# Attention results without transfers, and a new written order of the attention stage, in a one-core transformer block

## The chip, the cores and the metric

The kernel runs on one core of one Trainium2 chip. Its time is the device time of one launch, in microseconds (us), and the number compared is the median over several runs. A core has five instruction queues that work at the same time, each strictly in the order in which its program stands: TensorE (PE in the profile, with its weight loads as PEld), VectorE (DVE), ScalarE (ACT), GpSimd (POOL) and SyncE (SP). Here SP issues most of the DMA transfers. Matmul results land in PSUM, which DVE and ACT read; all other data lies in SBUF, or in DRAM between stages.

## What is computed

The input is one sequence of 1024 frames with 1024 features. One layer is computed in float32:

```
h = rms_norm(x, norm1);  proj = h @ w_in          -> q, k, v for 8 + 8 heads of 64, forget gates, gates
o_a = forgetting attention, 8 heads, causal:  softmax(q k^T/8 + c_t - c_s) v
o_b = band attention, 8 heads: own chunk of 64 frames and the 8 chunks before it, plus a learned bias by distance
merged = sigmoid(g_a) * (o_a @ w_branch_a) + sigmoid(g_b) * (o_b @ w_branch_b)
x = x + merged @ w_out
x = x + square(relu(rms_norm(x, norm2) @ w_up)) @ w_down
return rms_norm(x, final_norm)
```

## The kernel before

**Precision.** The matmuls take operands of the type F32R, so each float32 operand is split into a high half (a rounding copy, name ends in `h`) and a low half (the rest, name ends in `l`), and a product takes three matmuls: high by high, low by high, high by low. ACT makes high halves and DVE or POOL the low ones.

**Stages.** Projections of q, k, v and gates (to some 420 us), attention with pieces of the branch product laid into it (some 420 to 670 us), the rest of the branch product (to 717 us), the output product (to 793 us), and the two feed-forward products. The change touches only the attention and its two ends.

**Attention.** The sixteen heads run in the order of the list `HEADS`: number n = 0 to 7 are the eight forgetting ("fox") heads, 8 to 15 the eight band heads. Two heads that follow each other form a pair `pr`, and lie in rows 0 to 63 (`hh` = 0) and 64 to 127 (`hh` = 1) of one result tile. For a head there are eight chunks of 128 queries: scores into a PSUM tile `s` (there are two of these, used in turn), minimum over the keys on DVE into `mn`, exponential on ACT into `p<chunk>`. Then, for the two halves h of the queries, PE turns blocks of `p` (matmul against `ident`, into `pt`), ACT rounds them (`th`), DVE takes the low part (`tl`), and PE weighs the values with both into one PSUM tile `pv`. Rows 0 to 63 of `pv` hold the part from the low halves of the values, rows 64 to 127 that from the high halves; the result is their sum.

**The order** is written out by hand. Strings of letters stand for calls: `S` scores of the next chunk, `R` its minimum, `E` its exponential, `T` turn a group, `H` and `L` its two halves, `P` weigh it, `V` take the result out of `pv`, `F` one step of the branch product for the fox half of the heads ("filler": three matmuls), `M` the end of a group of four such steps, `O` the split of a finished band result. `FOX_HEAD` is the string of a fox head, `BAND_HEAD` of a band head (its F and M are left out before n = 9), `LAST_HEAD` of head 15, and `INTRO` moves the first letters of head 0 forward. Engines see the letters in this order, since the calls are kept in program order (`tc.keep_in_program_order`; SP's transfers called by `LO` too). `S`, `R`, `E` run one head ahead: while head n is turned and weighed, the chunks of head n + 1 are scored. The first chunks of head 0 are scored already between the last gate products, how many beside each is in `AHEAD`.

**The result of a half head** goes out in `evacuate`: ACT copies `pv` to `both`, SP sends rows 64 to 127 of it to the result tile `on` and rows 0 to 63 to the tile `lo`, so that both stand in the rows of the head. When a pair is whole, `done` adds `lo` to `on` for both halves on POOL, fetches the spread reciprocals of the softmax sums (`rb`, through DRAM: `reciprocals`, `spread_reciprocals`) and `normalise` multiplies. For fox pairs POOL also splits the product into `oh` and `ol`, which the fillers and the branch product read; band pairs go through DRAM (`o_dram`, back as `olt`), except the last one, which is split into `o3h` and `o3l`. Head 15 goes another way: ACT copies one half, DVE adds the other.

**The branch product's weights** for the band half (`ab_weight(0, c)`) are loaded and split after the written order, where the scheduler finds room.

Of the kernel before, what the change touches and what calls it, by code (L numbers as in the profile page):

```python
# [34 lines left out]
EARLY, AHEAD = 3, (0, 0, 0, 0, 2, 2, 2, 1)  # L35
# [5 lines left out]
INTRO = "THLPTHLTTHPHLL"  # L41
FOX_HEAD = "THSSRRETTSLPHEHTLSRTLPHERPHTSLTELSHVTPHRLRELTHSEPTSHLRPEPPLPHRLEPV"
BAND_HEAD = "FFTSFHTHFRLSLRMPETSHETPLFRHETSPLRHFVSTPEHLTRHPLLSFETFPRHLESPPSMRRVEE"
LAST_HEAD = "THLTHLFFFFMTHPPFLFFFMTPTHFLHFTFFPVLTMHPFHLTHFFFLPLOOOPOOMOPV"
# [47 lines left out]
def hybrid_block(ctx: ExitStack, tc: tile.TileContext, xT, xN, g1, wall, wf, fb, relb, g2, g3, outT):  # L92
# [567 lines left out]
    def make_scores():  # L660
        if len(made) == len(chunks):
            return
        n, i = chunks[len(made)]
        made.append(pss.tile([P, S], F32, tag="s", name="s"))
        score(n, i, made[-1], TO)
        if i == 7 and n + 2 < 16:
            load_head(n + 2, LO)
# [29 lines left out]
    oh = opool.tile([P, 4, S], F32R, tag="oh", name="oh")  # L697
    ol = opool.tile([P, 4, S], F32R, tag="ol", name="ol")
    o3h, o3l = [opool.tile([P, S], F32R, tag=t, name=t) for t in ("o3h", "o3l")]
# [25 lines left out]
    def fill():  # L725
# [28 lines left out]
        for n, (c, h) in enumerate(todo):  # L754
# [5 lines left out]
            for k in range(4):  # L760
                product(ps, k == 0, [((wh[:, k, :], wl[:, k, :]), (oh[:, k, hs(h)], ol[:, k, hs(h)]))], k < 3, TO)
# [32 lines left out]
    evac = []  # L794

    def weigh(n, h, js, first, last):
# [11 lines left out]
        if last:  # L808
            rows = slice(hh * HD, (hh + 1) * HD)
            if hh == 0:  # L810
                outs[pr, h] = ap0.tile([P, HALF], F32, tag="on", name=f"on{pr}_{h}", bufs=4)
                lows_o[pr, h] = ap0.tile([P, HALF], F32, tag="lo", name=f"lo{pr}_{h}", bufs=3)
            evac.append((n, h, pv))

    def evacuate():
            n, h, pv = evac.pop(0)
            pr, hh = HEADS[n]
            rows = slice(hh * HD, (hh + 1) * HD)
            if n == 15:
                AO.copy(lows_o[pr, h][rows], pv[0:HD])  # L820
                VO.tensor_tensor(outs[pr, h][rows], pv[HD:P], lows_o[pr, h][rows], op=ALU.add)
                done(n, h)
                return
            both = ap0.tile([P, HALF], F32, tag="both", name=f"both{n}_{h}", bufs=2)
# [3 lines left out]
            done(n, h)  # L828
            if n == 14:
                G.tensor_tensor(outs[pr, h][rows], outs[pr, h][rows], lows_o[pr, h][rows], op=ALU.add)  # L830
# [487 lines left out]
```

## Time and profile before

| what | us |
|---|---|
| median of 3 runs | 1441.51 (1438.96 to 1443.76) |
| profiled execution, its own time | 1437.3 |
| span of the profiled execution, first to last instruction | 1435.6 |
| PE busy in it | 1398.8 (97%) |
| DVE, ACT, POOL busy | 872.1, 698.1, 825.9 |
| mean granted clock of PE | 0.993 |

In the rows of the profile, `out<-in` names the tiles written and read, `x` gives a count of instructions in a row that groups several. In a timeline row the first number is the start in us from the start of the span, the second the length; a bracket at the end tells how long the engine sat idle before it and what ended that wait. In a row by stretches of time there stand the stretch, its length, then for PE, PEld, DVE, ACT and POOL the busy time and in brackets the instructions, then the clock that PE was granted (1.00 is full), the busy share of the DMA engines, and what they moved in GB/s. Matmuls overlap: the next one starts some time before the one ahead is shown to end, so what a matmul costs the queue is read from start to start.

### The profile page before, as it was taken

To read this page: it belongs to the slowest core of one execution; us is meant where nothing else is said; L and a number is where in the kernel's file an instruction comes from. 1 tells how busy PE (TensorE), PEld (TensorE's weight loads), DVE (VectorE), ACT (ScalarE), POOL (GpSimd) and SP (SyncE) were. 2 spreads that over 40 slices of the span, in tenths; PEclk is the share of its full clock that TensorE was granted. 3 is DMA by queue.
4 is the path that set the end of the run, shared out by engine and by line. 5 is a ranking of instruction groups with operands and counts; after the bars stand their busy time and mean duration, and the time that the engine had idled before them with its cause. 6 is when DMAs were issued, how large, how long until landed. Compare 5 with 4: busy or idle time off the path is not lost.

```text
span 1435.6 us, 20509 instructions
## 1 busy us (share of the span) xinstructions
PE 1398.8 (97%) x6658; PEld 1167.0 (81%) x6658; DVE 872.1 (61%) x1369; ACT 698.1 (49%) x1349; POOL 825.9 (58%) x650
## 2 busy tenths in 40 slices
PE   7999999999989999999999999999999999999996
PEld 5788888888878888887888788888888888888886
DVE  7756445543258886775655854554545558998644
ACT  8633333343348886764454543333343444444653
POOL 1377777779730433233833777777777546567563
PEclk9999999999999999999999999999999999999998
DMA  8447677773456898997644244444445784679263
GB/s 277 148 113 197 185 202 207 205 192 128 146 187 173 232 261 231 270 278 247 206 167 154 67 156 155 154 159 149 152 143 180 245 266 153 178 240 234 81 220 118
DMA packets 137622, 267.64 MB, mean 186 GB/s; under 512 B 19554, under 2 KB 21602, under 8 KB 134442
## 3 DMA queue, kind: packets, MB, share of 16 engines
q1 hardware_dynamic: 89658, 181.19, 41.0%
q10 hardware_dynamic: 44656, 77.26, 17.0%
q0 software_dynamic: 3200, 7.88, 2.5%
q8 instruction: 52, 0.85, 0.2%
q14 instruction: 56, 0.46, 0.1%
HBM read 172.70 MB, written 85.69 MB: 180 GB/s over the span
## 4 chain that ended last, share of the span: by engine, by line
PE 84%; DVE 4%; issue 3%; DMA 3%; POOL 2%; ACT 2%; SPq 1%; POOLq 0%; ACTq 0%; DVEq 0%
PE u L215 42%; PE dS L215 12%; PE dA L215 8%; PE o L215 5%; PE s L105 4%; PE m L215 3%; PE pt L105 3%; PE pv L105 3%; PE m L105 2%; PE u L105 1%; DMA wr<-wall 1%; DMA lo<-both 1%; DMA rb<-r_dram 1%; DVE s L105 1%; ACT th L105 1%
## 5 line engine op out<-in xcount | busy, mean ns | idle before, releaser
L164 POOL TENSOR_TENSOR wl_A<-wr,wh_A 128x512 fp32r<-128x512 f32 x118 | 158.5, 1352 | 90.5 <-ACT wh_A L162 75.0
L164 POOL TENSOR_TENSOR wl_S<-S,wh_S 128x512 fp32r<-128x512 f32 x102 | 136.2, 1338 | 30.9 <-ACT wh_S L162 30.3
L162 ACT CAST wh_S<-S 128x512 fp32r<-128x512 f32 x105 | 64.8, 621 | 115.4 <-PE u L215 58.7
L162 ACT CAST wh_A<-wr 128x512 fp32r<-128x512 f32 x105 | 64.9, 620 | 89.1 <-PE u L215 43.5
L905 POOL TENSOR_TENSOR on<-on,lo 128x512 f32<-128x512 f32 x14 | 18.0, 1288 | 156.8 <-DMA lo<-both 66.4
L105 DVE TENSOR_TENSOR tl<-pt,th 128x512 fp32r<-128x512 f32 (+1 forms) x144 | 91.0, 642 | 21.4 <-ACT th L105 20.6
L164 POOL TENSOR_TENSOR wl_S<-ks,wh_S 128x512 fp32r<-128x512 f32 x48 | 69.0, 1486 | 52.5 <-ACT wh_S L105 51.2
L105 ACT CAST th<-pt 128x512 fp32r<-128x512 f32 (+1 forms) x144 | 79.4, 554 | 35.0 <-PE pt L105 34.1
L578 DVE TENSOR_TENSOR u<-u,u 128x512 f32<-128x512 f32 x70 | 48.8, 697 | 75.8 <-PE u L215 73.2
L105 ACT ACTIVATE p<-s,mn 128x640 f32<-128x640 f32 (+4 forms) x121 | 85.9, 710 | 14.9 <-DVE mn L105 13.2
L105 PE MATMUL pt<-ident,p 128*128 128x128 f32 x528 | 81.0, 275 | 0.0
L185 POOL TENSOR_TENSOR S<-wr,wr 128x512 f32<-128x512 f32 x35 | 46.1, 1317 | 57.8 <-DMA wr<-wall 57.7
L105 PEld LDWEIGHTS pt<-ident,p 128*128 128x128 f32 x528 | 65.7, 142 | 11.1 <-issue 0.4
L164 POOL TENSOR_TENSOR wl_A<-ka,wh_A 128x512 fp32r<-128x512 f32 x32 | 45.8, 1439 | 35.6 <-ACT wh_A L105 34.3
L105 PE MATMUL pv<-th,v 128*128 128x512 f32 (+3 forms) x180 | 61.8, 353 | 3.1 <-ACT th L105 3.1
L277 ACT CAST qkh<-qk 128x512 fp32r<-128x512 f32 x32 | 19.9, 621 | 88.5 <-DMA sk_dram<-qkl 31.8
L105 PE MATMUL s<-qk 128*128 128x384 f32 (+2 forms) x192 | 60.5, 370 | 1.9 <-ACT p L105 1.8
L1073 ACT ACTIVATE v<-v 128x512 f32<-128x512 f32 x64 | 40.4, 632 | 44.6 <-DVE v L1072 42.1
L571 DVE TENSOR_TENSOR u<-u,c 128x512 f32<-128x512 f32 x35 | 24.5, 699 | 57.5 <-PE u L215 55.4
L105 PE MATMUL pv<-tl,v 128*128 128x512 f32 (+3 forms) x180 | 57.7, 339 | 1.3 <-DVE tl L105 1.3
L105 DVE CUSTOM_DVE_ANT_0 s<-s,bc 128x640 f32<-128x640 f32 (+2 forms) x64 | 42.3, 661 | 24.7 <-PE s L105 17.6
L1072 DVE SCALAR_TENSOR_TENSOR v<-u,rstd 128x512 f32<-128x512 f32 x64 | 43.9, 688 | 20.1 <-PE u L215 18.1
(437 smaller groups left out, 4703.6 us busy)
## 6 DMA issues: line engine op xcount, KB each, us to landing
wr<-wall SPq DMA_DIRECT2D x235, 256.0 KB, 3.5
a_dram<-at ACTq DMA_DIRECT2D x64, 256.0 KB, 2.0
xT<-a_dram SPq DMA_DIRECT2D x64, 256.0 KB, 4.1
qk<-qk_dram SPq DMA_DIRECT2D x15, 1024.0 KB, 5.3
qk_dram<-qkh ACTq DMA_DIRECT2D x96, 128.0 KB, 2.4
a_dram<-v ACTq DMA_DIRECT2D x48, 256.0 KB, 2.0
xB<-a_dram SPq DMA_DIRECT2D x44, 256.0 KB, 5.3
z_dram<-zt ACTq DMA_DIRECT2D x32, 256.0 KB, 2.5
```

Of the source, the lines that this page charges most:

```text
L105: return lambda *a, **kw: tc.keep_in_program_order(getattr(self.eng, name)(*a, **kw))
L162: (act.tensor_copy if act is G else act.copy)(wh, src)
L164: lows.append(eng.tensor_tensor(wl, src, wh.bitcast(F32), op=ALU.subtract))
L185: eng.tensor_tensor(t, raw(3), raw(2), op=ALU.add)
L215: done = eng.matmul(bank, w[wi], x[xi], start=(first and t == 0), stop=(t == n - 1 and not part), skip_group_check=part or not first)
L277: A.copy(dst[0], src)
L571: V.tensor_tensor(banks[1], banks[3], c22, op=ALU.add)
L578: V.tensor_tensor(banks[b], banks[b], u2, op=ALU.add)
L905: G.tensor_tensor(o, o, lows_o[pr, x], op=ALU.add)
L1072: V.scalar_tensor_tensor(v, src, 0.0, rstd[:, hs(h)], op0=ALU.max, op1=ALU.mult)
L1073: A.activation(v, v, AF.Square)
```

## The change

1. **No transfers of results.** `evacuate` is cut in two. `V` is one copy of 64 rows on ACT, which also moves them into the rows of the head; a new letter `X` (`evacuate_rest`) is the second step. For the first half (h = 0) of heads 0 to 13 that is a second ACT copy, into `lo`, and POOL adds the two later, once for a pair. For the second half, and for heads 14 and 15, ACT copies one half to `mv` and DVE adds the other straight from `pv`. The two transfers of each half head are gone.
2. **Reciprocals earlier.** They are taken at the first weighing of the pair's second head, fetched at its first half (with one transfer where there were two), and each half is normalised when it is there.
3. **The eighth chunk of head 0** is scored beside the seventh, ahead of the last gate product.
4. **New strings** for all four parts.
5. **Branch weights in the string.** A new letter `W` splits the first four weights of `ab_weight(0, c)` in the last head; they are loaded at filler steps 36, 40, 44 and 52.
6. `oh`, `ol`, `o3h`, `o3l` are one tile for each half, and the loads at the start of attention stand in another order (values of head 0 first, then heads 1 and 2).

```diff
-EARLY, AHEAD = 3, (0, 0, 0, 0, 2, 2, 2, 1)
+EARLY, AHEAD = 3, (0, 0, 0, 0, 2, 2, 2, 2)
-FOX_HEAD = "THSSRRETTSLPHEHTLSRTLPHERPHTSLTELSHVTPHRLRELTHSEPTSHLRPEPPLPHRLEPV"
+FOX_HEAD = "STTHRSETSHLRLREPTHLPTHESHLPVTRTELSRXHTLHSPEPHLTPTSHRLPEPHLRLESPRPVXE"
...
     def evacuate():
-            AO.copy(both, pv)
-            LO.dma_start(outs[pr, h][rows], both[HD:P])
-            LO.dma_start(lows_o[pr, h][rows], both[0:HD])
-            done(n, h)
+        if n == 15 and h:
+            normalise(pr, 0)
+        if h == 0 and n < 14:
+            AO.copy(outs[pr, h][rows], pv[HD:P])
+        else:
+            moved[n, h] = ap0.tile([P, HALF], F32, tag="mv", name=f"mv{n}_{h}", bufs=2)
+            AO.copy(moved[n, h][rows], pv[other])
+
+    def evacuate_rest():
+        n, h, pv = evac.pop(0)
...
+        if h == 0 and n < 14:
+            AO.copy(lows_o[pr][rows], pv[0:HD])
+        else:
+            VO.tensor_tensor(outs[pr, h][rows], pv[rows], moved.pop((n, h))[rows], op=ALU.add)
+        done(n, h)
...
     def spread_reciprocals(pr):
-        for hh in range(2):
-            LO.dma_start(rb[hh * HD:(hh + 1) * HD, :], r_dram[pr, hh:hh + 1, :].to_broadcast([HD, S]))
+        LO.dma_start(rb, r_dram[pr].rearrange("a (o s) -> a o s", o=1).to_broadcast([2, HD, S]))
...
+    load_values(0)
     load_head(1, LO)
-    load_values(0)
+    load_head(2, LO)
     load_values(1)
...
-        if js == order[0] and hh and h == int(n < 15):
+        if js == order[0] and hh and h == 0:
             reciprocals(pr)
...
-        elif h and hh:
-            for x in range(2):
-                o = outs[pr, x]
-                G.tensor_tensor(o, o, lows_o[pr, x], op=ALU.add)
-            spread_reciprocals(pr)
-            for x in range(2):
-                normalise(pr, x)
+        elif hh:
+            if h == 0:
+                o = outs[pr, h]
+                G.tensor_tensor(o, o, lows_o[pr], op=ALU.add)
+                spread_reciprocals(pr)
+            normalise(pr, h)
...
+        if fill_at in (36, 40, 44, 52):
+            c = len(branch_raw) + len([b for b, _ in ab_w if b == 0])
+            branch_raw.append(quarter(U_AB + c // 2, (0, 3)[c % 2], LO.dma_start))
...
+    def branch_weight():
+        AO.copy(wh, raw)
+        G.tensor_tensor(wl, raw, wh.bitcast(F32), op=ALU.subtract)
```

What the strings do to the queues is shown at two places; the names are the program's, with a running number behind a tile's name.

**PE at the start of attention.** `u7_3` is the last gate product (twelve matmuls), `s_4098` and `s_4034` are the scores of the eighth chunk of head 0. Before:

```order
L105 MATMUL u7_3_3682<-T4h_104,wl_7_A22_3918 128x512
L105 MATMUL s_4098<-qk0_3799 128x512 x2
L105 MATMUL s_4098<-sk0_3800 128x512 x2
L105 MATMUL pt_4110<-ident_66,p0_0_3943 128x128
L105 MATMUL pt_4110<-ident_66,p0_1_3949 128x128
L105 MATMUL pt_4110<-ident_66,p0_2_3971 128x128
L105 MATMUL pt_4110<-ident_66,p0_3_3977 128x128
L105 MATMUL pv_4119<-th_4111,v0_4094 128x512
L105 MATMUL pv_4119<-tl_4112,v0_4094 128x512
```

After the change, where the rows of `s_4034` stand before the first of the twelve matmuls of `u7_3`, and the last of these is followed by:

```order
L105 MATMUL u7_3_3682<-T4h_104,wl_7_A22_3918 128x512
L105 MATMUL pt_4114<-ident_66,p0_0_3943 128x128
L105 MATMUL pt_4114<-ident_66,p0_1_3949 128x128
L105 MATMUL pt_4114<-ident_66,p0_2_3971 128x128
L105 MATMUL pt_4114<-ident_66,p0_3_3977 128x128
L105 MATMUL pt_4121<-ident_66,p0_1_3949 128x128
L105 MATMUL pt_4121<-ident_66,p0_2_3971 128x128
L105 MATMUL pt_4121<-ident_66,p0_3_3977 128x128 x2
L105 MATMUL pt_4128<-ident_66,p0_2_3971 128x128
L105 MATMUL pt_4128<-ident_66,p0_3_3977 128x128
L105 MATMUL pv_4138<-th_4115,v0_4099 128x512
L105 MATMUL pv_4138<-tl_4116,v0_4099 128x512
```

The scores moved ahead of the gate product, and three turned groups stand before the first weighing, where it was one.

**PE where one fox head passes into the next.** `s_4257` and `s_4273` are the scores of the eighth chunk of the head that is being scored; the rows run from there. Before, the five weighings of the last five groups come behind it, of which the first four are:

```order
L105 MATMUL s_4257<-qk1_4087 128x512 x2
L105 MATMUL s_4257<-sk1_4088 128x512 x2
L105 MATMUL pv_4225<-th_4187,v0_4094 128x512
L105 MATMUL pv_4225<-tl_4188,v0_4094 128x512
L105 MATMUL pv_4225<-th_4199,v0_4094 128x512
L105 MATMUL pv_4225<-tl_4200,v0_4094 128x512
L105 MATMUL pv_4225<-th_4219,v0_4094 128x512
L105 MATMUL pv_4225<-tl_4220,v0_4094 128x512
L105 MATMUL pv_4225<-th_4236,v0_4094 128x384
L105 MATMUL pv_4225<-tl_4237,v0_4094 128x384
L105 MATMUL pv_4225<-th_4236,v0_4094 128x128
L105 MATMUL pv_4225<-tl_4237,v0_4094 128x128
```

After:

```order
L105 MATMUL s_4273<-qk1_4101 128x512 x2
L105 MATMUL s_4273<-sk1_4102 128x512 x2
L105 MATMUL pv_4230<-th_4240,v0_4099 128x384
L105 MATMUL pv_4230<-tl_4241,v0_4099 128x384
L105 MATMUL pv_4230<-th_4240,v0_4099 128x128
L105 MATMUL pv_4230<-tl_4241,v0_4099 128x128
L105 MATMUL pv_4230<-th_4249,v0_4099 128x256
L105 MATMUL pv_4230<-tl_4250,v0_4099 128x256
L105 MATMUL s_4297<-qk2_4108 128x128
L105 MATMUL s_4297<-sk0_3800 128x128
```

Only the last two groups are weighed behind the eighth chunk now; the first chunk of the next head (`s_4297`) follows, then two turned groups of four blocks, then the second chunk. Before, one turned group and the first chunk came behind the last weighing, and the second chunk right after.

**ACT at the same place**, one head later. `p_7` is the exponential of the eighth chunk. Before:

```order
L105 ACTIVATE p_6_4857,den_4705<-s,mn_4702 128x896
L105 CAST th<-pt 128x256
L105 ACTIVATE p_7_4871,den_4705<-s,mn_4702 128x1024
L105 COPY both_1_4877<-pv 128x512
L105 CAST th<-pt 128x512
L105 ACTIVATE p_0_4909,den_4705<-s,mn_4906 128x128
```

After:

```order
L105 CAST th<-pt 128x256
L105 ACTIVATE p_6_4850,den_4702<-s,mn_4697 128x896
L105 COPY mv_1_4870<-pv 64x512
L105 ACTIVATE p_7_4876,den_4702<-s,mn_4697 128x1024
L105 CAST th<-pt 128x512
L105 ACTIVATE p_0_4901,den_4702<-s,mn_4896 128x128
```

The copy out of `pv`, which waits for the last weighing, stands ahead of the eighth exponential now, and stood behind it.

More of the change, by code (lines that the diff above doesn't have):

```diff
@@ L696, in hybrid_block @@
     opool = pool(ostack, "opool", "left")
-    oh = opool.tile([P, 4, S], F32R, tag="oh", name="oh")
-    ol = opool.tile([P, 4, S], F32R, tag="ol", name="ol")
-    o3h, o3l = [opool.tile([P, S], F32R, tag=t, name=t) for t in ("o3h", "o3l")]
+    ohl = [[opool.tile([P, 4, HALF], F32R, tag=f"o{t}{h}", name=f"o{t}{h}") for t in "hl"] for h in range(2)]
+    o3 = [[opool.tile([P, HALF], F32R, tag=f"o3{t}{h}", name=f"o3{t}{h}") for t in "hl"] for h in range(2)]
     apq.append(pool(astack, "apq1", "right"))
@@ L792, in turn_p @@
         return pt[:, :x], th[:, :x], tl[:, :x]
-    evac = []
+    evac, moved = [], {}
     def weigh(n, h, js, first, last):
@@ L952, in branch @@
         wh, wl = ab_weight(0, c)
-        xs = [(oh[:, k, hs(h)], ol[:, k, hs(h)]) for k in range(3)] + [(o3h[:, hs(h)], o3l[:, hs(h)])]
+        xs = [(ohl[h][0][:, k, :], ohl[h][1][:, k, :]) for k in range(3)] + [o3[h]]
         product(ps, 0 in ks, [((wh[:, k, :], wl[:, k, :]), xs[k]) for k in ks], 3 not in ks)
```

60 lines of the change are left out of this document (29 added, 31 removed).

## The prediction

> **What bounds the kernel now.** I read the page's totals first, then the table by stretches of time, stage by stage.
>
> ```profile
> span 1435.6 us, 20509 instructions
> PE 1398.8 (97%) x6658; PEld 1167.0 (81%) x6658; DVE 872.1 (61%) x1369; ACT 698.1 (49%) x1349; POOL 825.9 (58%) x650
> ```
>
> PE is busy for 97% of the span, and the change takes no matmul away. So a gain can only come out of the 36.8 us in which PE sits idle, and out of time in which it runs at less than its full clock; a loss is a new wait of PE. By stretches, three places in the attention stage stand out:
>
> ```profile
> core 0: us, PE busy (x) PEld busy (x) DVE busy (x) ACT busy (x) POOL busy (x), PEclk, DMA share, GB/s
> 420.00:424.00 4.00, 1.03 (x7) 0.66 (x5) 2.30 (x4) 1.63 (x3) 0.00 (x0) 1.00 0.56 154
> 424.00:428.00 4.00, 3.36 (x19) 2.49 (x20) 2.27 (x4) 1.40 (x4) 0.00 (x0) 1.00 0.51 207
> 428.00:432.00 4.00, 3.29 (x14) 2.56 (x14) 2.20 (x9) 2.02 (x7) 0.00 (x0) 0.70 0.51 133
> 432.00:436.00 4.00, 4.00 (x27) 3.78 (x26) 3.09 (x7) 3.70 (x9) 0.00 (x0) 0.87 0.19 44
> 459.70:473.00 13.30, 13.14 (x86) 11.68 (x85) 11.43 (x29) 11.77 (x29) 7.46 (x7) 1.00 0.87 235
> 548.00:552.00 4.00, 1.03 (x6) 0.48 (x4) 1.39 (x2) 1.26 (x4) 4.00 (x5) 1.00 1.07 400
> 552.00:556.00 4.00, 3.83 (x15) 3.29 (x15) 1.68 (x5) 0.84 (x3) 2.60 (x3) 0.57 0.98 208
> 664.00:668.00 4.00, 3.22 (x17) 2.46 (x15) 0.88 (x2) 2.47 (x5) 1.84 (x2) 1.00 1.02 369
> 668.00:672.00 4.00, 1.59 (x7) 1.11 (x7) 4.00 (x4) 3.98 (x8) 2.30 (x2) 1.00 0.88 302
> 672.00:676.00 4.00, 3.83 (x10) 2.69 (x11) 3.87 (x8) 0.02 (x1) 0.00 (x0) 0.58 0.77 234
> ```
>
> Each place costs twice: the idle time, and then a stretch at about half the clock. Start of attention: idle 2.97 + 0.64 + 0.71 = 4.32, clock 4 x 0.30 + 4 x 0.13 = 1.72, together 6.0 us. First fillers: idle 2.97 + 0.17 = 3.14, clock 4 x 0.43 = 1.72, together 4.9. End of attention: idle 0.78 + 2.41 + 0.17 = 3.36, clock 4 x 0.42 = 1.68, together 5.0. That is 15.9 us on offer. The row from 459.70 is one fox head: PE 13.14 of 13.30, with ACT and DVE not far behind.
>
> **Start of attention (-4.0).** The rows of the three engines:
>
> ```profile
> 419.51 0.62 PE L105 MATMUL s<-qk 128*128 128x512 f32 x2
> 420.43 0.60 PE L105 MATMUL pt<-ident,p 128*128 128x128 f32 x4
> 421.05 1.22 DVE L105 CUSTOM_DVE_ANT_0 s<-s,wide 128x1024 f32<-128x1024 f32 x1
> 422.37 1.11 ACT L105 ACTIVATE p<-s,mn 128x1024 f32<-128x1024 f32 x1 [3.03 <-DVE mn L105]
> 424.10 0.49 PE L105 MATMUL pv<-th,v 128*128 128x512 f32 x1 [3.07 <-ACT th L105]
> 419.71 0.70 DVE L578 TENSOR_TENSOR u<-u,u 128x512 f32<-128x512 f32 x1 [0.96 <-PE u L105]
> 420.44 0.69 DVE L391 TENSOR_TENSOR zt<-u,rstd 128x512 f32<-128x512 f32 x1
> ```
>
> PE waits for `th`, which stands on ACT behind the eighth exponential, which waits for the eighth minimum, which waits for scores that PE has only just made. Scored before the last gate product, that chain of 1.32 (start of minimum to start of exponential) + 1.11 lies beside twelve gate matmuls, and `th` can start at once. Late next are the last gate's two DVE steps: the gate product ends 0.92 later (419.51 to 420.43, the scores that now stand ahead of it), so they end near 422.0, and the third turned group and the first `tl` stand behind them. That is about 1.2 of waiting; some 0.8 more I leave for the eight chunks of head 1, which are now scored with little else between. So 2.0 of 6.0 stay and no half-clock stretch. Ends: 1.7 gained (the clock alone) and 6.0.
>
> **First fillers (-4.9).**
>
> ```profile
> 550.39 0.50 PE L105 MATMUL m<-oh,wh_ab 128*128 128x512 f32 x1 [1.86 <-POOL oh L860]
> 552.17 0.55 PE L105 MATMUL m<-ol,wh_ab 128*128 128x512 f32 x1 [1.28 <-POOL ol L861]
> 547.28 2.51 POOL L855 TENSOR_TENSOR on<-on,rb 128x512 f32<-128x512 f32 x2 [0.94 <-DMA rb<-r_dram]
> rb<-r_dram SPq DMA_DIRECT2D x16, 256.0 KB, 6.9
> L105 SPq DMA_DIRECT2D on<-both x30: 461/477/605, 434.0 to 649.1; - x30
> ```
>
> PE waits for `oh` of the last fox pair, POOL for `rb`, and `rb` for an SP queue full of result transfers. With the change the reciprocals leave half a head earlier, and the first half is added and normalised in the middle of head 7: by the string some 6 us ahead of the head's end, with all of head 8 (about 13) before the first filler, against the 6.9 that `rb` takes to land in the median and four POOL steps of at most 1.3 (two took 2.51). I take the whole 4.9. Ends: 0 (if `rb` lands after all that) and 5.3.
>
> The transfers themselves (60 issues on SP, the 30 of `on` of 0.477 each in the median, and as many of `lo`) were on no other wait of PE, so I count nothing more for them. The four weight loads moved onto SP at steps 36 to 52 are issued in its program order, between result transfers that are gone: nothing.
>
> **End of attention (-4.4).**
>
> ```profile
> 669.87 0.45 PE L105 MATMUL s<-tl,v 128*128 128x384 f32 x1 [2.11 <-DVE tl L105]
> 665.46 1.31 ACT L162 CAST wh_ab<-wr 128x512 fp32r<-128x512 f32 x2 [2.80 <-DMA wr<-wall]
> ```
>
> The last `th` stands on ACT behind two weight splits that wait 2.80 for a load, and `tl` behind that. With `W` the loads are issued a head ahead, and the last two `th` stand ahead of what could still be late (the second set of `olt`, and the fourth `W` behind it). I leave 0.6 of the 5.0 for the last `tl` and the first split results. Ends: 0 gained and 5.0.
>
> **The seams of the fox heads (+6.0).** The price of the new order lies here. One seam now:
>
> ```profile
> 464.83 0.40 PE L105 MATMUL pv<-th,v 128*128 128x512 f32 x1
> 466.21 0.33 PE L105 MATMUL pv<-th,v 128*128 128x384 f32 x1
> 467.02 0.60 PE L105 MATMUL pt<-ident,p 128*128 128x128 f32 x4
> 467.37 0.31 PE L105 MATMUL s<-qk 128*128 128x128 f32 x1
> 467.51 0.27 PE L105 MATMUL s<-sk 96*128 96x128 f32 x1
> 467.71 0.39 PE L105 MATMUL s<-qk 128*128 128x256 f32 x1
> 468.05 0.82 PE L105 MATMUL pt<-ident,p 128*128 128x128 f32 x6
> 469.03 0.44 PE L105 MATMUL s<-qk 128*128 128x384 f32 x1 [0.16 <-ACT p L105]
> 466.45 1.12 ACT L105 ACTIVATE p<-s,mn 128x1024 f32<-128x1024 f32 x1 [0.32 <-DVE mn L105]
> 467.55 0.58 ACT L105 COPY both<-pv 128x512 f32<-128x512 f32 x1
> ```
>
> The scores of the eighth chunk leave PE at 464.83, and the second chunk of the next head takes the same tile of `s` as soon as the eighth exponential has read it: 467.57 ends ACT, 467.71 starts PE. That chain cannot be shorter than some 0.2 (PE to DVE) + 1.32 + 1.12 + 0.14 = 2.78. Now it is nearly covered: of the 2.88 from 464.83 to 467.71 PE waits about 0.14, and then about 0.45 for the third chunk (six turned blocks from 468.05 take 0.53, so it could start at 468.58). In the new order the cover is two weighings (466.21 to 467.02: 0.81), the first chunk (0.2) and two turned groups (0.35 each): 1.7. So PE waits 1.1, and for the third chunk, whose tile is freed by an exponential behind the eighth one and a rounding, about 0.35. Against 0.59 now, 0.85 more at each of seven seams between fox heads; the eighth, where the band chunks are shorter, little: 6.0 together. The ends: 0 (some other waits of a head vanish as the order shifts) and 10, if the copy out of `pv`, now ahead of the eighth exponential on ACT, adds its 0.58 each time. I take 6.0, by the row of the chain itself, which no other engine can shorten.
>
> **Added instructions.** Per head one ACT copy and one DVE add more, priced by head 15, which does this already:
>
> ```profile
> 671.44 0.58 ACT L105 COPY lo<-s 64x512 f32<-64x512 f32 x1
> 659.23 0.69 DVE L105 TENSOR_TENSOR on<-s,lo 64x512 f32<-64x512 f32 x1 [0.58 <-ACT lo L105]
> ```
>
> In a fox head ACT goes from 11.77 to 12.35 and DVE from 11.43 to 12.12 of 13.3: both stay under PE's 13.14, so beside the seams nothing. In the band heads with fillers PE has no wait to gain or lose: nothing. POOL drops adds that nobody on PE waits for.
>
> Sum: -4.0 - 4.9 - 4.4 + 6.0 = -7.3. The profiled execution took 1437.3 (span 1435.6), 4.2 below the median of 1441.51; I take the change off the median: 1441.5 - 7.3 = 1434.2, say **1434**.
>
> **The rivals.** *The seams cost nothing* beyond what they cost now: then -13.3, about 1428. For it: ACT and DVE have over 1 us to spare in a head. Against: the chain above is one of lengths, not of room.
>
> *A late transfer keeps one stall*: `rb` at the first fillers, or `olt` or a weight at the end. Then 4.4 to 4.9 is not gained: about -2.7, 1439, no measurable change (0.3%, or 4.3 us, is about what a measurement of this kernel can tell from none). For it: loads and results still share SP's queue, in which an issue waits for the one ahead. Against: the half head of lead.
>
> *Slower: the clock drops at the seams.* If a seam's waits bring on a half-clock stretch of 1.7 as at the three places, eight seams cost 13.6 more: -7.3 + 13.6 = +6.3, about 1448. It decides from five such stretches on. For it: the waits of a seam grow from 0.6 to about 1.45 us, within some 2.5 us. Against it: clocks fell behind 2.97 and 2.41 of idle in 4 us, and not behind this:
>
> ```profile
> 820.00:822.00 2.00, 0.93 (x5) 0.67 (x4) 2.00 (x9) 0.94 (x3) 2.00 (x2) 1.00 0.04 13
> ```
>
> The Trainium skill, "TensorE: Matmul & The Clock Gate", bears on this from two sides. Its Part 1 on the HAM clock gate states that the clock falls after an idle window of about 3.4 us: by that no seam would bring it down, and the sum stays -7.3; but the trace shows half clock after 1.86 and 1.28 of waiting with a matmul between, so it takes less than a full empty window. Its section "A second HAM failure mode: psum-queue depth-cycling" states that frequent short idle times between groups of matmuls make the clock swing: by that the sum would be +6.3. The trace does not bear it out: the fox heads now, with two waits at each seam, show 1.00.
>
> **How the numbers follow.** The forecast holds with 0.61 (its own range 1429 to 1437), no seam cost 0.15, one stall kept 0.15, clock drops 0.09. Faster by over 0.3%: 0.61 + 0.15 = 0.76; within: 0.15; slower: 0.09. The range takes in the first three cases with the ends of seams and stalls: 1425 to 1442.
>
> **What would show it.** Right: no stretch below full clock between 420 and 680; PE at the first fillers without a wait for `oh`; fox heads of about 14.1 us where now a head is 13.3, with PE waiting for `p` at the second chunk of each; no wait of ACT for `wr` at the end. Wrong: fox heads of 13.3 (seams covered) or of over 15 (clock), a wait for `rb` on POOL that reaches PE, or ACT waiting for `olt` ahead of a `th`.

## The result: 1478.5 us, slower by 2.5%, and the profile after

The changed kernel takes 1478.47 us (1475.98 to 1480.31) against 1442.33 for the kernel before on the same chip: ratio 1.0253, interval 1.0227 to 1.0279. The forecast was 1434 and its range ended at 1442. The first part of the profile after:

```profile
span 1474.3 us, 20382 instructions
PE 1415.2 (96%) x6658; PEld 1176.5 (80%) x6658; DVE 890.9 (60%) x1385; ACT 707.9 (48%) x1363; POOL 816.0 (55%) x641
```

PE does the same 6658 matmuls. It is idle for 1474.3 - 1415.2 = 59.1 us instead of 36.8, and takes 16.4 longer over them, in line with a lower mean clock (0.980 instead of 0.993). From the table of PE's waits in the kernel after (engine, line, released by; us in total, times, longest):

```profile
PE s L105 <- DMA sk<-sk_dram: 11.3, 6, 2.3
PE s L105 <- DMA qk<-qk_dram: 6.6, 4, 3.4
...
PE s L105 <- ACT p L105: 6.2, 9, 0.9
PE m L215 <- ACT wh_ab L105: 5.2, 1, 5.2
PE m L105 <- POOL wl_ab L745: 5.1, 3, 4.2
```

The wait for `oh` and `ol` at the first fillers is gone, as forecast. Four of these five lines are new, and they do not name the seams: they name head loads (`qk`, `sk`) and weight halves. The wait for `p` is the seams', and small. Of POOL's waits the longest in total is now this one:

```profile
POOL on L860 <- DMA rb<-r_dram: 127.3, 7, 23.6
```

Before, POOL waited 7.9 us for `rb` in all. The timeline of the kernel after around the first fox pair (SPq rows are issues on SP's queue):

```profile
448.05 0.58 SPq L105 DMA_DIRECT2D rb<-r_dram  x1
...
452.36 0.34 SPq L105 DMA_DIRECT2D qk<-qk_dram  x1
452.75 0.50 SPq L105 DMA_DIRECT2D sk<-sk_dram  x1
...
464.19 1.30 POOL L860 TENSOR_TENSOR on<-on,rb 128x512 f32<-128x512 f32 x1 [16.19 <-DMA rb<-r_dram]
...
469.39 0.30 PE L105 MATMUL s<-sk 96*128 96x128 f32 x1 [2.23 <-DMA sk<-sk_dram]
...
713.45 0.62 ACT L105 CAST oh<-olt 128x512 fp32r<-128x512 f32 x1 [11.10 <-DMA olt<-o_dram]
...
714.64 0.80 PE L215 MATMUL m<-oh,wh_ab 128*128 128x512 f32 x1 [5.21 <-ACT wh_ab L105]
```

`rb` is issued at 448.05 and POOL can use it at 464.19: 16 us, where the kernel before showed 6.9 in the median. `sk`, issued 4.7 us behind it, reaches PE only at 469.39. At the end the same happens to `olt` behind the last pair's `rb`, and ACT, which keeps its order, holds up `wh_ab` behind it. By stretches, with the DMA share and GB/s at the end of the row, two moments in which, by the issues on SP, `rb` was the only large transfer left to run:

```profile
449.00:452.00 3.00, 3.00 (x16) 2.56 (x15) 2.92 (x7) 2.00 (x5) 0.00 (x0) 1.00 0.11 44
481.00:484.00 3.00, 3.00 (x17) 2.50 (x15) 2.85 (x6) 2.05 (x5) 0.00 (x0) 1.00 0.12 42
```

A share of 0.11 to 0.12 is about two engines of 16 (0.125). The source of the new transfer is read by the pattern 2x64x1024 (two rows, each 64 times); before, each of the two transfers was read by 64x1024. The Trainium skill, "DMA: Bandwidth & Descriptors", section "Why a DMA increments its semaphore by 16 and not by 1", states that a transfer runs on the largest number of engines, up to 16, that divides the slowest dimension of both patterns, so a leading dimension of 2 leaves two. The trace agrees with its share of 0.11 to 0.12, and the runs below show what follows from it.

### The profile page after: what moved, and what is told of

Same layout as the page of the kernel before. It is cut to its first block, busy times and chain, and to the rows that moved or that the text cites. A ratio compares the mean times of both kernels' runs of the same rounds, so it can differ in the third digit from the quotient of the medians.

```text
span 1474.3 us, 20382 instructions
## 1 busy us (share of the span) xinstructions
PE 1415.2 (96%) x6658; PEld 1176.5 (80%) x6658; DVE 890.9 (60%) x1385; ACT 707.9 (48%) x1363; POOL 816.0 (55%) x641
## 3 DMA queue, kind: packets, MB, share of 16 engines
q1 hardware_dynamic: 84618, 173.32, 38.6%
## 4 chain that ended last, share of the span: by engine, by line
PE 73%; DMA 15%; DVE 5%; issue 4%; POOL 1%; ACT 1%; SPq 1%; POOLq 0%; ACTq 0%; DVEq 0%
PE u L215 42%; PE dS L215 8%; PE dA L215 7%; PE o L215 5%; DMA sk<-sk_dram 4%; DMA bc<-relb 3%; PE m L215 3%; PE s L105 2%; DMA rb<-r_dram 2%; PE pv L105 2%; PE pt L105 2%; DMA wr<-wall 2%; DMA xT<-a_dram 1%; DMA v<-v_dram 1%; PE u L105 1%
## 5 line engine op out<-in xcount | busy, mean ns | idle before, releaser
L105 ACT ACTIVATE p<-s,mn 128x640 f32<-128x640 f32 (+3 forms) x120 | 84.2, 702 | 22.0 <-DVE mn L105 21.1
L860 POOL TENSOR_TENSOR on<-on,rb 128x512 f32<-128x512 f32 x14 | 17.7, 1275 | 127.3 <-DMA rb<-r_dram 127.3
L105 PE MATMUL s<-sk 96*128 96x384 f32 (+2 forms) x192 | 55.5, 343 | 11.3 <-DMA sk<-sk_dram 11.3
```

Source lines behind the costliest of these rows:

```text
L105: return lambda *a, **kw: tc.keep_in_program_order(getattr(self.eng, name)(*a, **kw))
L860: G.tensor_tensor(o, o, rb, op=ALU.mult)
```

## The experiments

All times are medians, ratios are to the kernel before on the same chip. The kernels ran on several chips, so small differences between them are to be read from the ratios. "Head" is the mean distance between the first scores of heads 2 to 8, six fox heads, read from the timeline.

| kernel | us | ratio (interval) | head | POOL's wait for `rb` |
|---|---|---|---|---|
| before | 1441.5 to 1443.6 | 1 | 13.25 | 7.9 |
| after | 1478.5 | 1.0253 (1.0227 to 1.0279) | 15.58 | 127.3 |
| after, two `rb` transfers | 1433.8 | 0.9939 (0.9920 to 0.9958) | 14.21 | 44.9 |
| before, one `rb` transfer | 1509.4 | 1.0470 (1.0444 to 1.0496) | 15.57 | 82.9 |
| after, `rb` cut by columns | 1474.7 | 1.0232 (1.0208 to 1.0256) | 15.64 | 102.1 |
| after, `rb` issued by POOL | 1503.6 | 1.0424 (1.0397 to 1.0451) | 14.20 | 154.8 |
| two transfers, pattern 4x16x1024 | 1463.5 | 1.0139 (1.0120 to 1.0159) | 14.32 | 99.8 |
| two transfers, old order | 1434.7 | 0.9942 (0.9924 to 0.9960) | 14.49 | 47.5 |
| two transfers, old order, GpSimd adds | 1425.4 | 0.9879 (0.9863 to 0.9896) | 13.24 | 25.6 |
| two transfers, new order, GpSimd adds | 1430.6 | 0.9920 (0.9897 to 0.9942) | 14.03 | 34.0 |
| two transfers, start undone | 1434.0 | 0.9925 (0.9901 to 0.9949) | 14.21 | 41.6 |
| two transfers, late reciprocals | 1434.8 | 0.9955 (0.9937 to 0.9972) | 14.36 | 79.5 |
| two transfers, no W | 1434.1 | 0.9950 (0.9934 to 0.9966) | 14.21 | 43.0 |
| two transfers, old order, late reciprocals | 1434.9 | 0.9932 (0.9909 to 0.9955) | 14.48 | 77.4 |
| two transfers, GpSimd adds, other strings | 1425.1 | 0.9889 (0.9866 to 0.9913) | 13.77 | 36.8 |
| **two transfers, old order, GpSimd adds, short intro** | **1422.0** | **0.9843 (0.9811 to 0.9875)** | 13.25 | 41.8 |
| the same, late reciprocals | 1426.4 | 0.9884 (0.9865 to 0.9902) | 13.25 | 49.6 |

### The `rb` transfer

**Undone alone**, in the changed kernel:

```diff
-        LO.dma_start(rb, r_dram[pr].rearrange("a (o s) -> a o s", o=1).to_broadcast([2, HD, S]))
+        for hh in range(2):
+            LO.dma_start(rb[hh * HD:(hh + 1) * HD, :], r_dram[pr, hh:hh + 1, :].to_broadcast([HD, S]))
```

> The changed kernel with one thing undone: rb is loaded by two transfers of 64x1024 again, one for each head of the pair, in place of one whose outermost dimension is 2. Theory A (the single transfer has only two DMA engines to run on, and the loads queued behind it come late): PE's waits for sk and qk (17.9 us together) and POOL's for rb (127.3 us) go nearly all, the fox heads are all 14.0 to 14.4, and the time is 1432 to 1445. Rival B (the new order and the extra ACT and DVE work are the loss): 1470 to 1480. Rival C (SP's issues wait in order for r_dram and for POOL, whatever the shape): 1465 to 1480, with the waits for sk and qk still there.

1433.8. Two lines gave 3.1% back, and PE has no wait for `qk` or `sk` left. The span of its profile is 1433.5 us. The same place in its timeline:

```profile
451.52 1.09 SPq L105 DMA_DIRECT2D rb<-r_dram  x2
...
456.25 1.28 POOL L861 TENSOR_TENSOR on<-on,rb 128x512 f32<-128x512 f32 x1 [4.95 <-DMA rb<-r_dram]
```

4.7 us from issue to use, where the single transfer took 16.

**Done alone**, in the kernel before (the same two lines, the other way round):

> The kernel before with one thing added: its two rb transfers are made one with an outermost dimension of 2. Everything else, strings and result transfers, is that of before. Theory A: rb takes about 16 us to land where its median was 6.9, the head loads behind it come late, the first fillers wait some 9 us longer, and the time is 1452 to 1475. Rivals B and C: 1438 to 1446, as before.

1509.4, more than expected: in the kernel before the result transfers stand behind `rb` on SP too. Two of PE's waits:

```profile
PE pv L105 <- ACT both L105: 16.8, 3, 7.4
PE m L105 <- POOL oh L859: 13.9, 1, 13.9
```

The result transfers of `both` come back late (ACT waits 25.3 us for them in all), ACT cannot copy `pv`, PE cannot write it. PE also waits 17.9 for `th`, which ACT makes, and the first fillers wait 13.9 where they waited 1.9.

**The shape, or the number of transfers?** Two transfers of 128x512, each by 2x64x512:

```diff
+        for h in range(2):
+            LO.dma_start(rb[:, hs(h)], r_dram[pr, :, hs(h)].rearrange("a (o s) -> a o s", o=1).to_broadcast([2, HD, HALF]))
```

> The changed kernel with two rb transfers again, but cut by columns: each is 128x512 with the outermost dimension of 2 kept. It tells the shape from the number of transfers. Theory A, by the shape: each half takes about 8 us and they follow one another, so the head loads are as late as in the changed kernel; the first half is there earlier for POOL: 1465 to 1480. If it is the number or the size of the transfers (A by size): as with two transfers by heads, 1432 to 1445. Rival B: 1470 to 1480.

1474.7, by its interval not told apart from the single transfer. It is not the number.

**Four engines.** Rows, bytes and issues as in the kernel with two transfers, only the pattern written as 4x16x1024:

```diff
-            LO.dma_start(rb[hh * HD:(hh + 1) * HD, :], r_dram[pr, hh:hh + 1, :].to_broadcast([HD, S]))
+            LO.dma_start(rb[hh * HD:(hh + 1) * HD, :],
+                         r_dram[pr, hh:hh + 1, :].rearrange("(b a) s -> b a s", b=1).to_broadcast([4, HD // 4, S]))
```

> The kernel with two rb transfers of 64x1024, each read by an access pattern of 4x16x1024 in place of 64x1024; rows, bytes, issues and place are the same. Theory A (the outermost dimension sets how many DMA engines work): the pair runs on four engines, takes about half of the 16 us of the single transfer, POOL's waits for rb come to 60 to 90 us (44.9 with two, 127.3 with one), and the time is 1437 to 1458. If only the number or the rows of a transfer matter: 1431 to 1437, POOL's waits near 45.

1463.5. The same addresses in the same order of rows, only grouped otherwise, cost 2%. The DMA share while only `rb` runs is now that of four engines of 16 (0.25), and POOL's wait lies between:

```profile
452.00:453.00 1.00, 1.00 (x8) 0.91 (x7) 0.84 (x4) 0.78 (x1) 0.00 (x0) 1.00 0.24 53
479.00:481.00 2.00, 2.00 (x11) 1.66 (x10) 1.85 (x4) 1.05 (x4) 0.00 (x0) 1.00 0.24 45
```

The packets of SP's queue fit this. For the same bytes its page counts 84618 with 2 in front, 84666 with 4 and 84858 with 64, so 48 and 240 more. That is what comes out if each transfer ends with one packet for each engine that it runs on: 8 transfers on 2 engines (16), 16 on 4 (64), 16 on 16 (256).

That the pattern sets the engines, and that it costs the time, is so shown; the size was underrated (99.8 and 1463.5, where 60 to 90 and at most 1458 were expected). The 99.8 are six waits; a seventh of 12.4, at the first pair, the profile puts down to `qk`. Twice the engines did not halve the time: the rows show 53 and 45 GB/s where two engines moved 44 and 42, and the first `rb` takes 12.3 us from issue to use (448.69 to 460.94), where one transfer took 16 and two wide ones 4.7. Why four engines moved hardly more than two no run here shows.

**From another queue.** The single transfer, issued by POOL:

```diff
-        LO.dma_start(rb, ...to_broadcast([2, HD, S]))
+        G.dma_start(rb, ...to_broadcast([2, HD, S]))
```

> The changed kernel with the single rb transfer, its shape unchanged, issued by POOL in place of SP. POOL has to wait for it in any case. Theory A with the loss by loads queued behind it on the same queue: PE's waits for sk and qk go, POOL still waits some 100 us or more for rb, and the time is 1440 to 1458. Theory A with the loss by the two engines themselves being taken (whatever queue the transfer came from): waits for sk and qk stay, 1465 to 1480. Rival C (SP's issues waiting in order for r_dram): 1440 to 1450 with POOL's waits for rb small.

1503.6, outside every expectation. PE's waits for `sk` and `qk` from DMA go, as the first theory had it, but `rb` itself is slower still. The transfers of this kernel, with the median from issue to landing at the end:

```profile
qk<-qk_dram SPq DMA_DIRECT2D x15, 1024.0 KB, 9.0
...
rb<-r_dram POOLq DMA_DIRECT2D x8, 512.0 KB, 23.6
```

And POOL, which waits for `rb` in its order, makes others late, by the waits of PE:

```profile
PE m L105 <- POOL wl_ab L745: 31.6, 4, 15.3
PE s L105 <- POOL sk L480: 18.8, 1, 18.8
```

`sk` L480 is a memset of POOL that stands behind `rb`. The median of `qk` is 9.0 here, against 5.6 with two transfers, though it no longer stands behind `rb` on its queue. So what is lost depends on who stands behind the transfer. Why it is slower still from here is open: this run changes a second thing. POOL's queue carries the 4.2 MB of all eight `rb` in 8320 packets of about 0.5 KB, where SP's queue took 1040 of about 4 KB. How much of `qk`'s delay is due to shared DMA engines was not measured apart.

### The seams

With two transfers a fox head takes 14.21; forecast was 14.1, before 13.25. One seam of that kernel:

```profile
470.44 1.06 PE L105 MATMUL pt<-ident,p 128*128 128x128 f32 x8
472.17 0.39 PE L105 MATMUL s<-qk 128*128 128x256 f32 x1 [0.67 <-ACT p L105]
```

Read from start to start, as the prediction did, the second chunk stands 1.73 behind two turned groups of 0.35 each, so it waits 1.03 (forecast 1.1). The third chunk, at 473.00, waits about 0.35 in the same way (forecast 0.35). Is that the order, or the new way out of `pv`? Four kernels, two by two. The old order means the strings of the kernel before, with `X` behind each `V`; "GpSimd adds" means that `pv` is read once, by one ACT copy, and the rest is on POOL:

```diff
-INTRO, FOX_HEAD = (new)
+INTRO = "THLPTHLTTHPHLL"
+FOX_HEAD = "THSSRRETTSLPHEHTLSRTLPHERPHTSLTELSHVXTPHRLRELTHSEPTSHLRPEPPLPHRLEPVX"
```
```diff
 V:  +            AO.copy(both, pv)                                    # 128 rows; heads 0 to 13
 X:  +            G.tensor_copy(mv[rows], both[other])
     +            G.tensor_tensor(outs[pr, h][rows], both[rows], mv[rows], op=ALU.add)
```

> The kernel with two rb transfers, and the order of the fox heads and of the intro put back to that of the kernel before (the eighth chunk of a head scored five weighings before the seam); X stands right behind each V, so the new evacuation of pv stays. Theory S (the 0.9 us of each seam come from scoring the eighth chunk beside the seventh, as the prediction has it): fox heads 13.3 to 13.5, time 1426 to 1431. Rival V (they come from pv, which is now read twice, one copy after the other, before the next weighing may write it): fox heads 13.9 to 14.2, time 1431 to 1438.

> The kernel with two rb transfers in the new order, with pv read only once and the half moved and added on GpSimd. Theory S: the seams still wait for the eighth exponential, fox heads 13.9 to 14.3, time 1431 to 1437. Rival V: fox heads 13.3 to 13.5, time 1426 to 1430.

> As the run with the old order, and pv is read only once, by one ScalarE copy of 128x512; X moves the half between rows on GpSimd (copy of 64x512) and adds there. By theory S and by rival V alike the fox heads come back to 13.2 to 13.4, and the time is 1425 to 1430, 1.0 to 1.2% under the kernel before. If GpSimd, which waits in order for rb, gives the two buffers of the copy back late, ScalarE waits for them: over 1435.

Neither edit alone brings the seams back: 14.49 with the old order alone (outside both expectations), 14.03 with GpSimd alone, 13.24 with both. The wait of PE at one seam in the timeline of the old order alone:

```profile
499.41 0.44 PE L105 MATMUL s<-qk 128*128 128x384 f32 x1 [0.98 <-ACT p L105]
```

The same in the new order with GpSimd's add:

```profile
499.09 0.38 PE L105 MATMUL s<-qk 128*128 128x256 f32 x1 [0.77 <-ACT p L105]
```

And in the old order with GpSimd's add:

```profile
481.97 0.44 PE L105 MATMUL s<-qk 128*128 128x384 f32 x1 [0.15 <-ACT p L105]
```

The 0.77 for the second chunk in the new order is the chain of the prediction: the eighth chunk is scored too late to be covered. The old order has no such wait, but another one of about 1.0 for the third chunk, when the added copy and add stand on ACT and DVE. Its cause stands in DVE's queue at the same seam:

```profile
497.92 0.68 DVE L105 TENSOR_TENSOR on<-pv,mv 64x512 f32<-64x512 f32 x1 [1.67 <-ACT mv L105]
```

DVE waits for ACT's copy ahead of the minimum of the next head's first chunk, so that chunk's exponential is late, and with it the tile of `s` that the third chunk takes. Rival V's own mechanism, PE waiting to write `pv`, shows only once, with 0.27 us, in head 0. With both gone 0.15 stays, as before. POOL has the time for it: its adds and copies for this take 36.0 and 17.0 us in the fastest kernel of the table.

### The start, the first fillers and the end

With two transfers, the stretches of the start:

```profile
420.00:424.00 4.00, 3.12 (x18) 2.26 (x17) 2.54 (x4) 2.08 (x5) 0.00 (x0) 1.00 0.73 232
424.00:428.00 4.00, 3.47 (x16) 3.09 (x17) 2.31 (x4) 1.73 (x5) 0.00 (x0) 0.73 0.66 231
428.00:432.00 4.00, 3.35 (x18) 2.52 (x16) 1.24 (x5) 2.61 (x7) 0.00 (x0) 0.85 0.73 197
432.00:436.00 4.00, 3.11 (x12) 2.97 (x12) 2.96 (x9) 2.90 (x7) 0.00 (x0) 0.58 0.00 0
436.00:440.00 4.00, 4.00 (x23) 3.30 (x22) 3.45 (x6) 2.71 (x7) 0.00 (x0) 0.99 0.01 4
```

Idle 0.88 + 0.53 + 0.65 + 0.89 = 2.95, clock 4 x (0.27 + 0.15 + 0.42 + 0.01) = 3.40: 6.4 us, where the kernel before lost 6.0. **The eighth chunk** behind the last gate product again, in that kernel:

```diff
-EARLY, AHEAD = 3, (0, 0, 0, 0, 2, 2, 2, 2)
+EARLY, AHEAD = 3, (0, 0, 0, 0, 2, 2, 2, 1)      # and S, R, E ahead of INTRO
```

> The kernel with two rb transfers, with one part undone: the eighth chunk of the first head is scored, and its minimum and exponential taken, after the last gate product again, as in the kernel before. If this part is worth the 4.0 us of the prediction: 1436 to 1440. If it is worth nothing (the windows of the run with two rb transfers show as much lost between 420 and 440 as before, 6.4 of 6.0): 1432 to 1436.

In this form of it head 2's load stood ahead of the eighth scores in program order, so that they were made from head 2's operands and waited 7.9 us for them: 1443.3, which tells nothing of the part. With that load behind the scores:

> The start undone again, now with head 2's load behind the eighth scores of head 0, as in the kernel before (in the first try it stood ahead of them, and they waited for it). If the part is worth the 4.0 us of the prediction: 1436 to 1440. If nothing: 1432 to 1436, with 5 to 6.5 us of idle and clock lost between the last gate product and some 16 us behind it, as in the run with two rb transfers.

1434.0 against 1433.8, with intervals that lie on each other: the part is worth nothing that can be measured. Its stretches give idle 1.84 + 0.79 + 0.65 + 0.87 = 4.15 and clock 4 x (0.30 + 0.13) = 1.72, together 5.9:

```profile
420.00:424.00 4.00, 2.16 (x15) 1.70 (x13) 2.59 (x4) 1.16 (x3) 0.00 (x0) 1.00 0.84 229
424.00:428.00 4.00, 3.21 (x13) 2.80 (x14) 2.25 (x4) 1.86 (x5) 0.00 (x0) 0.70 0.74 288
428.00:432.00 4.00, 3.35 (x21) 2.78 (x19) 1.03 (x6) 2.74 (x7) 0.00 (x0) 0.87 0.39 114
432.00:436.00 4.00, 3.13 (x18) 2.42 (x17) 3.53 (x9) 3.20 (x9) 0.00 (x0) 1.00 0.16 31
```

**Other strings**, for a start in which PE has head 1's first scores to make while the last gate's DVE steps run:

```diff
+INTRO = "THTST"
+FOX_HEAD = "TSRSHERTLTSHPLEHRTSTHLRPPESHTLELVXRTTHLSHEPTRHESLLPSTHRRELPHPPPLEPVX"
```

> The run with the old order and GpSimd's add (1425.4), with a shorter intro (THTST) and another fox order: the first scores of head 1 are issued while the last gate's DVE steps still hold up th, and the seams have six weighings behind the last score. What is left there: 3.2 us of idle and 1.7 of clock at 420 to 436, and 1.7 of idle over the seven fox heads to 540, together 6.6. If half of it goes: 1420 to 1424. If the first head's scores only move the wait for th, or the clock drops all the same: 1424 to 1428.

1425.1: no gain over 1425.4, because these strings make the fox head 13.77. Its granted clock stays at 1.00 over the whole start, though, so the short intro was tried with the old fox order:

```diff
-INTRO = "THLPTHLTTHPHLL"
+INTRO = "THTST"
```

> The run with the old order and GpSimd's add (1425.4) with its intro cut to THTST, and nothing else changed: the fox order of 13.25 a head with the start of the other strings. If the start keeps what it showed there (1.4 us of idle and no clock lost, against 3.2 and 1.7): 1420 to 1423.5. If it is bound to the fox order of those strings: 1424 to 1427.

1422.0, the fastest kernel here, 1.6% under the one before (its interval overlaps that of 1425.4). Its start loses 1.14 us between 420 and 428, with no stretch below full clock, where the kernel of 1425.4 lost 3.2 of idle and 1.7 of clock:

```profile
420.00:424.00 4.00, 2.86 (x21) 2.33 (x20) 3.27 (x9) 2.72 (x9) 0.00 (x0) 1.00 0.98 344
424.00:428.00 4.00, 4.00 (x31) 3.82 (x30) 3.54 (x11) 3.59 (x10) 0.19 (x1) 1.00 0.54 123
```

What moves the start is thus not the eighth chunk but what PE has to do while `th` is not there. And `th` waits for the last gate's DVE steps, as the timeline of the kernel of 1425.4 shows, with the eighth exponential done 1.4 us earlier:

```profile
421.07 1.12 ACT L520 ACTIVATE p<-s,mn 128x1024 f32<-128x1024 f32 x1 [0.64 <-DVE mn L509]
...
423.55 0.58 ACT L105 CAST th<-pt 128x512 fp32r<-128x512 f32 x1 [1.28 <-DVE zt L391]
```

**Late reciprocals**, in the kernel with two transfers, then in the one with the old order, then in the fastest:

```diff
-        if js == order[0] and hh and h == 0:
+        if js == order[0] and hh and h == int(n < 15):
             reciprocals(pr)
 ...
-        elif hh:                       # done: spread at h == 0, normalise each half when it is there
+        elif hh and h:                 # spread, then normalise both halves, at the pair's end
```

> The kernel with two rb transfers, with one part undone: the reciprocals leave half a head later and both halves of a pair are normalised at its end, as in the kernel before. If the early halves are what took the stall of the first fillers away (4.9 us): the wait of PE for oh and ol comes back, with a stretch below full clock behind it, 1437 to 1441. If the shorter SP queue alone does it: 1432 to 1436.

> The run with the old order (1434.7) with the reciprocals half a head later as well, so that of the kernel before's attention only the result transfers are gone and W and the eighth chunk stay changed. If the missing transfers alone took the stall of the first fillers away: no wait of PE for oh or ol, full clock from 540 to 570, 1432 to 1437. If the order or the early half did: the waits for oh and ol are back, 1438 to 1442.

> The kernel of 1422.0 (old fox order, short intro, GpSimd's add) with the reciprocals half a head later and both halves of a pair normalised at its end, as in the kernel before. With slow seams that delay cost nothing, but there PE came to the first fillers some 9 us later than in the kernel before. If only that lateness hid it: PE waits for oh and ol at the first fillers again, about 540 to 550, by 3 to 8 us, with a stretch below full clock, and the time is 1425 to 1431 (ratio to the kernel before 0.987 to 0.991). If the missing result transfers are enough: no wait, 1420 to 1424 (0.983 to 0.986).

1434.8 and 1434.9: no loss, no wait for `oh` or `ol`. But with fast seams 1426.4 against 1422.0 (the intervals of the ratios overlap a little), and the stall is back in the timeline and the stretches:

```profile
544.06 0.49 PE L105 MATMUL m<-oh,wh_ab 128*128 128x512 f32 x1 [0.53 <-POOL oh L868]
...
546.66 0.79 PE L105 MATMUL m<-ol,wh_ab 128*128 128x512 f32 x1 [2.10 <-POOL ol L869]
```

```profile
540.00:544.00 4.00, 3.53 (x23) 2.95 (x20) 1.99 (x6) 3.68 (x10) 4.00 (x5) 1.00 0.86 326
544.00:548.00 4.00, 1.84 (x5) 1.34 (x6) 0.73 (x2) 0.00 (x0) 3.85 (x6) 0.81 1.02 262
548.00:552.00 4.00, 4.00 (x22) 3.42 (x22) 2.65 (x7) 2.00 (x6) 2.32 (x2) 0.76 0.90 274
```

Idle 0.47 + 2.16 and clock 4 x (0.19 + 0.24): 4.35 us, which agrees with the 4.4 that the kernel lost. In the first two kernels PE reaches the fillers 7 to 10 us later than in the kernel before, which hides the stall there; in the third it comes 4.4 us earlier. But the third kernel differs in one more thing: GpSimd's add and copy stand on POOL ahead of `ol`:

```profile
542.17 1.29 POOL L834 TENSOR_TENSOR on<-both,mv 64x512 f32<-64x512 f32 x1
...
544.63 0.61 POOL L833 COPY mv<-both 64x512 f32<-64x512 f32 x1
```

These 1.9 us are most of the 2.6 that PE waits. So the 4.4 are the price of late reciprocals together with GpSimd's add; what they cost with fast seams alone was not tried.

**No `W`** (its letters and loads left out; the weights are split after the written order again):

> The kernel with two rb transfers, with one part undone: the four weight halves of the first branch products are loaded and split where they are first used, as in the kernel before, not by W inside the last head. If W took the stall at the end of the attention away (4.4 us): 1436 to 1440, with ACT's wait for wr and PE's for tl or th near 665 to 675. If not: 1432 to 1436.

1434.1: no measurable loss. The waits come back in part (`tl` 0.76 and 1.10, ACT for `wr` 2.42 and 0.98), without the half-clock stretch:

```profile
671.33 0.44 PE L105 MATMUL s<-tl,v 128*128 128x384 f32 x1 [1.10 <-DVE tl L105]
```

## Why the prediction was wrong, point by point

**The step that failed** is the price of `rb` in "first fillers": "against the 6.9 that `rb` takes to land in the median". That row is of two transfers read by 64x1024; the change makes it one read by 2x64x1024, and the text on the change says so, but the prediction gave this edit no term and no reason for leaving it out. It was worth +45 (1478.5 against 1433.8), more than all terms together. The rival "a late transfer keeps one stall" had the right kind of cause and a tenth of its size: it took a late transfer to hit one place, while POOL waited for this one in seven of eight pairs, with the next head's loads on the same queue behind it. Three of the signs that would show it wrong came. The wait for `rb` on POOL reaches PE through `wl_ab`: at the sixth pair POOL waits 23.6 us for `rb`, and PE then 4.2 for the `wl_ab` made behind it. ACT waits 11.1 for `olt`, though a weight half stands behind it and not a `th`. And fox heads take over 15, but mostly by waits for late loads; the clock, which the prediction had named beside it, was 0.95 to 0.97 from 440 to 530, by an estimate 0.6 us of the 2.3 that a head grew.

**The seams (+6.0)** were right in size and, in this order, in mechanism: 14.21 - 13.25 over seven seams is +6.7, with PE waiting for `p` at the second chunk. Not right is that they are the price of the order alone. That the added instructions cost nothing nearly holds in the new order (14.21 against 14.03); in the old one the same copy and add cost 14.49 - 13.24 = 1.25 a head.

**The start (-4.0)** was wrong: 0. With two transfers the start loses 6.4 of 6.0. The step that the prediction named as late next, the last gate's DVE work, was priced about right: 1.2 of waiting, where the timeline shows 0.64 + 0.54 + 0.22 = 1.40. The 0.8 left for the chunks of head 1 came to 0.65 + 0.89 = 1.54. What failed most is "no half-clock stretch": after these waits the clock fell, and cost 3.40 where it had cost 1.72. The lower end given for the gain, 1.7 for the clock alone, should have been 0.

**The first fillers (-4.9)** came (no idle there with two transfers), but without early reciprocals it did not come back either, as long as the seams were slow. Two terms that were added hang together: with slow seams the early half is worth 0, with fast ones and GpSimd's add 4.4.

**The end (-4.4)** came (0.19 idle left from 660 to 680 with two transfers), about 1.9 of it from `W` by the waits that come back without it, though the time does not show them (1434.1 against 1433.8); of the rest no part was tried alone.

**The clock at the seams**, the slower rival: no. With two transfers the stretches show full clock with a wait at every seam:

```profile
440.00:475.00 35.00, 32.60 (x206) 28.10 (x205) 30.16 (x74) 30.56 (x71) 7.64 (x7) 1.00 0.59 177
475.00:530.00 55.00, 52.13 (x326) 44.67 (x325) 48.04 (x107) 48.82 (x113) 17.18 (x16) 1.00 0.61 173
```

The prediction quoted the Trainium skill, "TensorE: Matmul & The Clock Gate", section "A second HAM failure mode: psum-queue depth-cycling", on this; here waits of 0.6 to 0.8 at each seam, and of 0.9 to 1.1 in the old order, did not make the clock swing.

**The sum without `rb`** fits: 1433.8 against 1434.2. Most of that is luck. By stretches the kernel with two transfers loses 6.4 at the start where it was 6.0, and gains 4.9 and 4.8 against 6.7 at the seams: about -2.6, and the spans of the two profiled executions differ by 2.1; the medians differ by 7.8 (interval 6.0 to 11.5). The profiled execution of the kernel before was 4.2 under its own median, that of the other one 1.4 above.

What the stretches leave out is the clock of the other launches. The profiled launch of the kernel before had a mean granted clock of 0.993; in its seven launches on the chip of the kernel with two transfers the middle value is 0.991, and that kernel's is 0.995. An estimate: against the profiled launches that is 0.002 of 1399 us of matmuls, 2.8 us, more for the one, and 0.001, 1.4 us, less for the other; with the 2.1 of the spans it makes 6.3 of the 7.8. Over the 22 launches of the kernel before on another chip the time falls as the clock rises, from 1446.1 us at 0.986 to 1439.0 at 0.993. So part of the gain is clock that no term of the sum names. Where in the kernel the other launches lose it no profile here shows, and that stays open.

## What to carry to other kernels

Price a transfer by a row of the same pattern, not of the same bytes: look at the outermost dimension of both sides, above all where a broadcast puts a small count in front, and look for stretches in which one transfer runs alone at a small DMA share. A slow transfer costs what stands behind it, on its queue and on the engine that waits for it in order. Terms of a sum are not independent when one delays the engine that another makes wait: a stall "gained" next to a new delay must be priced both with and without that delay. And before the stretches of one profiled launch are taken for the kernel, its clock should be held against that of the other launches.

## What the runs showed of the hardware that was not expected

The pattern of a transfer's source sets how many of the 16 DMA engines work: a share of 0.11 to 0.12 with 2 in front, 0.24 with 4, and POOL's waits of 127.3, 99.8 and 44.9 us with 2, 4 and 64 in front. Between 4 and 64 the rows, bytes and issues are the same. The time does not go with the number of engines alone: four moved 45 to 53 GB/s, two 42 to 44.

The clock does not follow the length of a wait alone. The two kernels with the old order have the same waits behind the last gate product, 2.06 for `th` and 0.22 for `tl`. In the stretch behind that, the one without GpSimd's add, then the one with it:

```profile
424.00:428.00 4.00, 2.98 (x20) 2.28 (x19) 2.40 (x7) 2.08 (x6) 0.00 (x0) 1.00 0.71 159
```

```profile
424.00:428.00 4.00, 3.59 (x14) 2.89 (x14) 1.47 (x3) 1.11 (x4) 0.00 (x0) 0.59 0.75 244
```

One keeps its full clock, the other falls to 0.59. The Trainium skill, "TensorE: Matmul & The Clock Gate", Part 1, states that activity is judged in free-running windows of about 3.4 us, which would fit a result that depends on when the wait falls, though no run here shows that this is the cause; its idle window of that whole length is more than the 2.06 that sufficed here.
